# Feed-forward: the first products of two gate pairs ahead of four plain tiles made whole

## The chip, the cores and the metric

The kernel runs on one core of a Trainium2 chip. The time is device microseconds of one execution; the table below gives the median of three runs. The profile is of one further execution, whose own time stands beside its span.

The engines are named as the profile names them: PE (TensorE matmul), PEld (its weight load), DVE (VectorE), ACT (ScalarE), POOL (GpSimd) and SP (SyncE, which here only issues DMAs).

## What is computed

A small decoder trunk in float32: 512 tokens, width 1024, two layers (a short convolution, then windowed attention), and behind each a SwiGLU feed-forward of width 2816. The change lies in the feed-forward, which both layers run:

```python
def swiglu(h, w_gate_up, w_down):
    g, u = jnp.split(h @ w_gate_up, 2, axis=-1)
    return (jax.nn.silu(g) * u) @ w_down

ff = swiglu(rmsnorm(h, ffn_pre_norm[l]), ffn_w_gate_up[l], ffn_w_down[l])
h = h + rmsnorm(ff, ffn_post_norm[l])
```

## The kernel before

**Split numbers.** Every float32 operand of a matmul is split into a high part (ACT, a copy to fp32r) and a low part (DVE, the difference). A product is then three matmuls, hi·lo, hi·hi and lo·hi (`mm3`, L207 to L210). Where a token tile holds its high and low half side by side (`both`), one matmul of 512 columns does hi·[hi|lo], and one of 256 does lo·hi; the two halves of the PSUM bank are added afterwards. A weight block is 128x1024; it is loaded by SP into one of 7 `raw` buffers and split once.

**Tiles and pairs.** The 2816 gate and 2816 up columns are cut into 22 tiles of 128. The first two are "plain" (`PLAIN = 2`): two gate and two up tiles, each a sum over eight k-blocks of the normalised tokens. The other 20 come as ten pairs `q`. A pair is computed by a seven-product scheme: the 2x2 blocks of weights and tokens are combined so that seven block products (numbered 1 to 7) on 256 tokens each do for eight. Product 1 uses the first four k-blocks of the first 256 tokens, product 2 the last four of the same tokens; 6, 5, 7, 3 and 4 use sums of token quarters (`factors`, L389), for which all 512 tokens are needed.

**A pair in the code.** `gate_jobs` (L1203) makes seven jobs in the order 1, 2, 6, 5, 7, 3, 4. Products 1, 6, 7, 4 accumulate in the same two PSUM banks (chain X), one for each of two output tiles; 5 and 3 in Z; 2 in Y. Behind each product `take` (L1230) reads the bank: after product 1 ACT copies one half and DVE adds the other (`st`, 2 + 2 operations of 256 columns), after 6 the same, after 7 four DVE adds, after 4 two copies, two adds and two multiplies of 512; after 5 one ACT copy; after 2 and 3 one DVE add of 512. So product 6 adds onto the banks in which product 1 stands, and `take` reads the running sum. Matmuls of the next product of a chain must wait until `take` has read the bank. At pair 0 the first two products' weights were split beforehand.

**The order.** Everything in the feed-forward runs under a schedule written by hand: PE, DVE, ACT and POOL take their instructions in the order of the program. `in_line` (L505) runs the jobs: run job j (PE, then `take`), split the weights of job j + 3, add the raw blocks of job j + 4 where a pair's sums aren't ready made (L488), and emit one of the late parts. Late parts are the six steps by which a finished gate pair is turned into operands of the down projection (`pair_sums`, L601). Jobs of the first down projection take none at first. Ready-made sums of weight blocks are accumulated in HBM by POOL's DMAs (`sum_on`).

**The opening of a layer.** The stage before ends with the last token tile's norm, which is a long chain over DVE, POOL and ACT, and PE needs work that uses only the first 256 tokens until tiles 2 and 3 are done. `last_tile` (L1132) writes out that chain, with splits of the first tokens (`split`), copies of token quarters (`keep`) and two early weight splits (`weights`, in half blocks) between. `project_first` (L1158) gives PE its work: the four plain tiles on the first 256 tokens, k by k, then on the last 256. Between its k-blocks stand the transposes of tiles 2 and 3 (`turn`), the splits and copies of the last 256 tokens, and `factors`. After it, `late` closes the plain tiles (`gate_pair`: silu on ACT, multiply on DVE) and the jobs of the pairs begin.

```python
for hf in range(2):                                  # 256 tokens each
    for ks in ((0, 1), *((k,) for k in range(2, KT))):
        for ps, (whi, wlo) in zip(pss, ws):          # four plain tiles
            for k in ks:
                mm3(ps[:, c], ...)                   # N = 256
        for k in ks:
            then(hf, k)                              # turns, splits, factors
```

**Weights ahead.** `Ahead` holds the weights split before the layer begins: four are split while the stage before closes (`one`, whole blocks), two in `last_tile` (`slots`). Before, `first_weights` names the four of the plain tiles and then the two of pair 0's products 1 and 2.

Of the kernel before, what the change touches and what calls it, by code (L numbers as in the profile page):

```python
# [12 lines left out]
AF = mybir.ActivationFunctionType  # L13
ALU = mybir.AluOpType
PSUM = bass.MemoryType.PSUM

P = 128
# [5 lines left out]
ROUNDS = [(0, 6), (6, 10), (10, 14), (14, 18), (18, 22)]  # L23

PLAIN = 2

ADDED = (1, 2, 3, 4, 5, 7)

# [55 lines left out]
def yoco_kernel(  # L84
# [43 lines left out]
    def slot(s, dt=F32, w=S):  # L128
        return big.tile([P, w], dt, tag="slot", name=name(s), padded_shape=[P, S])
# [127 lines left out]
    class Update:  # L257
# [128 lines left out]
                else:  # L386
                    nc.scalar.activation(out, src, AF.Copy, scale=gain)

        def factors(self):  # L389


            x = self.x[0]
            made = {p: [] for p in range(1, 8)}
            for p, k0, c in ((1, 0, 0), (2, 4, 0), (3, 4, 256)):
                made[p] = [[a[:, c : c + 256] for a in x[k0 + k]]
                           + [two[:, :, c : c + 256] for two in self.both[k0 + k :][:1] if two]
                           for k in range(4)]
            for j in range(2):
                q11, q21, q12, q22 = (self.parts[i, hf, j] for hf in range(2) for i in range(2))

                nc.vector.tensor_tensor(out=q11, in0=q11, in1=q12, op=ALU.subtract)
# [730 lines left out]
    def last_tile(res, pieces, ahead=None):  # L1132


        def some(i):
            for n, *f in pieces[i]:
                if n == "keep":
# [20 lines left out]
    def project_first(pss, ws, x, then):  # L1158
        for hf in range(2):
            c = slice(hf * 256, (hf + 1) * 256)  # L1160

            for ks in ((0, 1), *((k,) for k in range(2, KT))):
                for ps, (whi, wlo) in zip(pss, ws):
                    for k in ks:
                        kk = slice(k * P, (k + 1) * P)
                        mm3(ps[:, c], whi[:, kk], wlo[:, kk],
                            x[k][0][:, c], x[k][1][:, c], k == 0, k == KT - 1)
                for k in ks:
                    then(hf, k)
# [12 lines left out]
    def ffn(l, before, ahead, gain, gpres, following):  # L1182
# [5 lines left out]
        def gate_pair(pg, pu):  # L1188
# [11 lines left out]
            pair.clear()  # L1200
            return pair_sums(gr, acts[0])

        def gate_jobs(q, factors, out, to, then):  # L1203


# [13 lines left out]
            split = {}  # L1219
            if q == 0:  # L1220

                pools = {"X": ps_sc, "Y": ps_pt, "V": ps_pt, "Z": ps_mm}
                raws[1], raws[2] = [], []
                split = {1: ahead.ready[4], 2: ahead.ready[5]}
            banks, kept = {}, []

            def tiles(a):
                return a.rearrange("p (e c) -> p e c", e=2)

            def take(p):  # L1230
                x, y, z, v = (banks.get(c) for c in "XYZV")
                st, u, gr = kept
                g0, g1 = (gr.rearrange("p (e h c) -> p e h c", e=2, h=2)[:, :, h]
                          for h in range(2))

                def add(out, a, b):
                    nc.vector.tensor_tensor(out=out, in0=a, in1=b, op=ALU.add)  # L1237
# [29 lines left out]
            def run(p):  # L1267
                def products(job):
                    if not kept:
                        kept.extend([slot("st"), slot("st"), wide("gr")])  # L1270
                    whi, wlo = split[p] if p in split else job.w
                    c = chain[p]
                    opened = c not in banks
                    if opened:
# [23 lines left out]
            def end():  # L1298
# [44 lines left out]

        acts = [[] for _ in ROUNDS]
        mix = [None] * NB
        pss = [bank("pgu", ps_mm) for _ in range(4)]
        with tc.manual_schedule(engines=ALL):
            last_tile(before, [
                [(0, 4)], [(0, 5), ("keep", 0, False), ("weights",)],
                [], [("keep", 1, True), (0, 6), (0, 7), ("keep", 3, True)],  # L1350
                [("keep", 2, False), ("weights",)]], ahead)

            def then(hf, k):
                if hf == 0 and k in (5, 6):
                    for b in ((0, 1), (2, 3))[k - 5]:
                        before.turn(b, (2,))
                if hf == 0 and k == 6:
                    for b in range(4):
                        before.turn(b, (3,))
                    for f in range(KT):  # L1360
                        before.split(0, f, 1)
                    for b in range(4):
                        before.keep(b, 1)
                if hf == 1 and k == 1:
                    factors.update(before.factors())
                if hf == 1 and k == 3:
                    if l == 0:
                        sum_on("o1")
                    sum_on(f"{l}f0")

            factors = {}
            project_first(pss, ahead.ready[:4], xs, then)

            def late():
                parts = [gate_pair(*pss[i : i + 2]) for i in (0, 2)][1]
                sum_on(f"{l}f1")
                return parts
# [568 lines left out]
```

## Time and profile before

| | |
|---|---|
| median of 3 runs | 1010.17 us (1009.65 to 1010.23) |
| the profiled execution | 1010.16 us, of which the span is 1008.3 us |
| mean granted TensorE clock | 0.998 |
| first feed-forward opens (first matmul of a plain tile) | 176.7 us, in layer 1 494.3 us later |

A profile line of a group reads: line, engine, operation, output <- inputs, shapes, count, then busy time and mean duration in ns of one, then the idle time before it and what ended that. A line of the timeline reads: start and duration in us, engine, line, operation, count, and in brackets the idle time before it with its releaser. Rows of several like instructions are merged (x8), and a duration overlaps the start of the next instruction, so that the step from start to start is what one costs on its engine. Line numbers such as L1237 are lines of the kernel; L1237 is the `add` inside `take`, L501 the low half of a weight split, L500 its high half, L192 and L198 the same for half blocks, L369 and L370 high and low of a token split, L387 a `keep`, L401 to L412 `factors`.

### The profile page before, as it was taken

How to read it: one execution, taken by the hardware profiler on the slowest of the kernel's cores; microseconds unless marked ns; L12 is line 12 of the kernel's file. 1: busy time of each engine (PE TensorE's matmuls, PEld its weight loads, DVE VectorE, ACT ScalarE, POOL GpSimd, SP SyncE). 2: the span in 40 equal slices, each digit the busy share in tenths (PEclk: the TensorE clock that was granted, in tenths of full speed). 3: DMA queues.
4: the chain of work that ended last, by engine and by line, in shares of the span. 5: the costliest groups of instructions: out<-in, count | busy, mean ns of one | idle time of the engine just before them, and what ended most of it. 6: DMA issues, size and time to landing. Idle time of an engine off the chain costs nothing. (4 is left out here: it accounts for less than half of the span.)

```text
span 1008.3 us, 16460 instructions
## 1 busy us (share of the span) xinstructions
PE 999.5 (99%) x6008; PEld 887.4 (88%) x6008; DVE 911.2 (90%) x1564; ACT 609.5 (60%) x1105; POOL 184.6 (18%) x250
## 2 busy tenths in 40 slices
PE   9999999999999999999999999999999999999997
PEld 8899888999889898898898888799998988989986
DVE  7898877899799999999888998989997999999996
ACT  7445545875655455566485788777666564646641
POOL 0211021212101011000022756321201010110001
PEclk9999999999999999999999999999999999999999
DMA  9885988669979699779504889966999587978742
GB/s 342 266 253 172 335 291 289 200 198 286 342 236 298 225 301 317 241 217 333 198 1 136 216 241 250 278 259 170 311 281 315 167 253 239 300 259 271 244 169 83
DMA packets 67872, 246.61 MB, mean 245 GB/s; under 512 B 8016, under 2 KB 8784, under 8 KB 56016
## 3 DMA queue, kind: packets, MB, share of 16 engines
q1 hardware_dynamic: 52624, 148.14, 39.5%
q0 software_dynamic: 14592, 96.48, 37.6%
q8 instruction: 47, 0.77, 0.3%
q10 hardware_dynamic: 576, 0.95, 0.3%
q14 instruction: 33, 0.27, 0.1%
HBM read 239.25 MB, written 102.76 MB: 339 GB/s over the span
## 5 line engine op out<-in xcount | busy, mean ns | idle before, releaser
L501 DVE TENSOR_TENSOR wlo<-raw,whi 128x1024 fp32r<-128x1024 f32 (+1 forms) x231 | 279.0, 1212 | 26.5 <-ACT whi L500 26.3
L500 ACT ACTIVATE whi<-raw 128x1024 fp32r<-128x1024 f32 (+1 forms) x231 | 239.7, 1051 | 79.1 <-DVE raw L488 37.6
L1282 PE MATMUL gx<-xt,whi 128*128 128x512 f32 x480 | 120.6, 393 | 0.0
L1282 PEld LDWEIGHTS gx<-xt,whi 128*128 128x128 f32 x480 | 86.2, 189 | 15.7
L571 POOL DMA_DIRECT2D hsum<-in_w_gb_dram x96 | 63.7, 727 | 160.8 <-ACT whi L500 107.5
L571 POOL DMA_DIRECT2D hsum<-hsum x32 | 25.3, 790 | 351.5 <-ACT whi L500 257.7
L1260 ACT ACTIVATE st<-gx 128x256 f32<-128x256 f32 x120 | 43.5, 380 | 60.8 <-PE gx L1285 57.2
L1237 DVE TENSOR_TENSOR st<-gx,st 128x256 f32<-128x256 f32 x200 | 77.4, 417 | 2.2 <-ACT st L1260 0.4
L1285 PEld LDWEIGHTS gx<-xt,wlo 128*128 128x128 f32 x480 | 65.5, 190 | 4.7
L1285 PE MATMUL gx<-xt,wlo 128*128 128x256 f32 x480 | 66.9, 282 | 0.0
L1296 ACT ACTIVATE gr<-gr 128x1024 f32<-128x1024 f32 x20 | 21.2, 1062 | 55.8 <-DVE gr L1237 55.8
L208 PE MATMUL gy<-xlo,whi 128*128 128x256 f32 x176 | 49.8, 283 | 0.0
L209 PE MATMUL gy<-xhi,whi 128*128 128x256 f32 x176 | 49.8, 283 | 0.0
L210 PE MATMUL gy<-xhi,wlo 128*128 128x256 f32 x176 | 49.8, 283 | 0.0
L208 PE MATMUL px<-wlo,ahi 128*128 128x512 f32 x120 | 46.7, 389 | 0.0
L209 PE MATMUL px<-whi,ahi 128*128 128x512 f32 x120 | 46.7, 389 | 0.0
L210 PE MATMUL px<-whi,alo 128*128 128x512 f32 x120 | 46.7, 389 | 0.0
L571 POOL DMA_DIRECT2D hsum<-in_w_dn_dram x48 | 32.1, 765 | 69.0 <-ACT whi L500 47.4
L1282 PE MATMUL gx<-xhl,whi 128*128 128x512 f32 x160 | 39.9, 391 | 0.0
L672 DVE TENSOR_TENSOR mix<-mix,px 128x512 f32<-128x512 f32 x54 | 34.8, 679 | 2.1 <-PE px L210 2.1
L318 POOL TENSOR_TENSOR ur<-uv,mhalf 128x1 f32<-128x1 f32 x15 | 13.9, 928 | 115.0 <-DVE uv L313 114.9
L488 DVE TENSOR_TENSOR raw<-raw,raw 128x1024 f32<-128x1024 f32 x28 | 34.1, 1218 | 0.1
(359 smaller groups left out, 3052.4 us busy)
## 6 DMA issues: line engine op xcount, KB each, us to landing
hsum<-in_w_gb_dram POOLq DMA_DIRECT2D x96, 512.0 KB, 8.0
raw<-hsum SPq DMA_DIRECT2D x88, 512.0 KB, 8.1
raw<-in_w_gb_dram SPq DMA_DIRECT2D x60, 512.0 KB, 7.1
hsum<-in_w_dn_dram POOLq DMA_DIRECT2D x36, 512.0 KB, 8.0
raw<-in_w_dn_dram SPq DMA_DIRECT2D x32, 512.0 KB, 7.0
hsum<-hsum POOLq DMA_DIRECT2D x28, 512.0 KB, 5.6
hsum<-in_w_dn_dram POOLq DMA_DIRECT2D x12, 768.0 KB, 13.0
raw<-in_w_in_dram SPq DMA_DIRECT2D x13, 512.0 KB, 7.2
```

Of the source, the lines that this page charges most:

```text
L208: nc.tensor.matmul(out, whi, xlo, start=start, stop=False, **kw)
L209: nc.tensor.matmul(out, whi, xhi, start=False, stop=False, **kw)
L210: nc.tensor.matmul(out, wlo, xhi, start=False, stop=stop, **kw)
L488: nc.vector.tensor_tensor(out=raw, in0=raw, in1=self.raws[1].tile, op=ALU.add)
L500: self.begun = nc.scalar.activation(hi[:, :n], raw, AF.Copy)
L501: nc.vector.tensor_tensor(out=lo[:, :n], in0=raw, in1=hi[:, :n].bitcast(F32), op=ALU.subtract)
L571: nc.gpsimd.dma_start(dst, src, max_dma_last_dim=4 * 4 * S, **kw))
L672: nc.vector.tensor_tensor(out=m, in0=m, in1=banks[bs][r], op=ALU.subtract if half else ALU.add)
L1237: nc.vector.tensor_tensor(out=out, in0=a, in1=b, op=ALU.add)
L1260: nc.scalar.activation(ste, a, AF.Copy)
L1282: nc.tensor.matmul(banks[c][e], whi[:, kk], factors[p][k][2], start=opened and k == 0, stop=False, **kw)
L1285: nc.tensor.matmul(banks[c][e][:, :256], wlo[:, kk], factors[p][k][0], start=False, stop=k == 3 and p in (4, 5), **kw)
```

## The change

Four weights are ready when the layer begins; now they are blocks 0 and 1 of pairs 0 and 1 (products 1 and 2), and the four of the plain tiles come later. PE's work on the first 256 tokens is now products 1 and 2 of both pairs (`Opening`), kept in four banks that hold product 1 and then product 1 + 2. Copies and adds bring these sums into SBUF (`st` and one half of `gr`). The plain tiles become four jobs at the head of the line, each made whole with 512 columns. The jobs of pairs 0 and 1 begin at product 6, in fresh banks, and `take` adds `st` where the bank no longer holds product 1.

```diff
+OPENED = 2
-        def factors(self):
+        def factors(self, between):
...
                     made[p] += [[hi[:, c : c + 256], lo[:, c : c + 256], two[:, :, c : c + 256]]
                                 for c in (0, 256)]
+                if j == 0:
+                    between()
             return made
...
     def first_weights(l):
-        return ([w_gu[l, f, j] for f in range(2) for j in range(2)]
-                + [w_gb[l, 0, b] for b in range(2)])
+        return ([w_gb[l, q, b] for b in range(2) for q in range(OPENED)]
+                + [w_gu[l, f, j] for f in range(PLAIN) for j in range(2)])
...
+        class Opening:
+            def __init__(self, q):
+                self.ws = ahead.ready[q], ahead.ready[OPENED + q]
+                self.x = [bank("gx", ps_mm) for _ in range(2)]
+                self.st, self.gr = slot("st"), wide("gr")
+
+            def one(self, k):
+                whi, wlo = self.ws[0]
+                for e, ps in enumerate(self.x):
+                    kk = slice(e * S + k * P, e * S + (k + 1) * P)
+                    nc.tensor.matmul(ps, whi[:, kk], before.both[k][:, :, :256], start=k == 0,
+                                     stop=False, skip_group_check=True)
+                    nc.tensor.matmul(ps[:, :256], wlo[:, kk], xs[k][0][:, :256], start=False,
+                                     stop=False, skip_group_check=True)
+
+            def two(self, *ks):
+                whi, wlo = self.ws[1]
+                for k in ks:
+                    for e, ps in enumerate(self.x):
+                        kk = slice(e * S + (k - 4) * P, e * S + (k - 3) * P)
+                        mm3(ps[:, :256], whi[:, kk], wlo[:, kk],
+                            *(a[:, :256] for a in xs[k]), False, k == KT - 1,
+                            skip_group_check=True)
+
+            def to(self, second, e):
+                return (self.gr[:, e * S : e * S + 256] if second
+                        else self.st[:, e * 256 : (e + 1) * 256])
+
+            def copy(self, second):
+                for e, ps in enumerate(self.x):
+                    nc.scalar.activation(self.to(second, e), ps[:, :256], AF.Copy)
+
+            def add(self, second):
+                for e, ps in enumerate(self.x):
+                    out = self.to(second, e)
+                    nc.vector.tensor_tensor(out=out, in0=ps[:, 256:], in1=out, op=ALU.add)
...
-                if p == 2:
+                if early and p == 6:
+                    both = slot("st")
+                    kept.append(both)
+                    for e in range(2):
+                        c = slice(e * 256, (e + 1) * 256)
+                        add(both[:, c], x[e][:, :256], st[:, c])
+                        add(both[:, c], x[e][:, 256:], both[:, c])
+                elif early and p == 5:
+                    add(u, z, st)
+                elif early and p == 3:
+                    add(g1, tiles(z), tiles(kept[3]))
+                elif early and p == 4:
+                    for e in range(2):
+                        c = slice(e * 256, (e + 1) * 256)
+                        add(st[:, c], x[e][:, :256], st[:, c])
+                        add(st[:, c], x[e][:, 256:], st[:, c])
+                elif p == 2:
                     add(g0, tiles(y), tiles(st))
...
-                    for p in (1, 2, 6, 5, 7, 3, 4)]
+                    for p in (1, 2, 6, 5, 7, 3, 4)[2 if early else 0 :]]
...
-        pss = [bank("pgu", ps_mm) for _ in range(4)]
         with tc.manual_schedule(engines=ALL):
+            ahead.fetch(2)
+            opened_pairs = first, second = [Opening(q) for q in range(OPENED)]
+            for pair_of in opened_pairs:
+                for k in range(4):
+                    pair_of.one(k)
             last_tile(before, [
-                [(0, 4)], [(0, 5), ("keep", 0, False), ("weights",)],
-                [], [("keep", 1, True), (0, 6), (0, 7), ("keep", 3, True)],
+                [(0, 4)],
+                [(0, 5), ("keep", 0, False), ("do", lambda: first.copy(False)),
+                 ("do", lambda: first.add(False))],
+                [("do", lambda: second.copy(False))],
+                [("keep", 1, True), (0, 6), (0, 7), ("keep", 3, True),
+                 ("do", lambda: second.add(False))],
                 [("keep", 2, False), ("weights",)]], ahead)
...
+            first.two(4, 5)
+            second.two(4, 5)
+            for b in range(2):
+                before.turn(b, (2,))
+            first.two(6, 7)
+            for b in range(2, 4):
+                before.turn(b, (2,))
+            for b in range(4):
+                before.turn(b, (3,))
+            first.copy(True)
+            first.add(True)
+            second.two(6, 7)
+            for f in range(KT):
+                before.split(0, f, 1)
+            ahead.slots()
+            second.copy(True)
+            second.add(True)
+            for b in range(4):
+                before.keep(b, 1)
+            ahead.one()
+            factors = before.factors(ahead.one)
+
+            pss = []
+
+            def plain_job(n):
+                def run(job):
+                    pss.append(bank("pgu", ps_mm))
+                    project(pss[n], ahead.ready[2 * OPENED + n], xs)
+
+                def then():
+                    if n == 0:
+                        if l == 0:
+                            sum_on("o1")
+                        sum_on(f"{l}f0")
+                    if n == 1:
+                        sum_on(f"{l}f1")
+                    return gate_pair(*pss[n - 1 :]) if n % 2 else None
+
+                return Job([], run, then)
...
-            jobs, behind_one = [], []
+            jobs, behind_one = [plain_job(n) for n in range(2 * PLAIN)], []
```

`project_first`, its `then` and the old `late` are removed; `project` (three matmuls of 512 columns for each of eight k-blocks) is the kernel's own, unchanged.

More of the change, by code (lines that the diff above doesn't have):

```diff
@@ L1136, in some @@
             for n, *f in pieces[i]:
-                if n == "keep":
+                if n == "do":
+                    f[0]()
+                elif n == "keep":
                     res.keep(f[0], 0, f[1])
@@ L1156, in last_tile @@
         some(4)
[L1158 to L1169, printed above, removed]
     def first_weights(l):
-        return ([w_gu[l, f, j] for f in range(2) for j in range(2)]
-                + [w_gb[l, 0, b] for b in range(2)])
+        return ([w_gb[l, q, b] for b in range(2) for q in range(OPENED)]
+                + [w_gu[l, f, j] for f in range(PLAIN) for j in range(2)])
     sum_on("o0")
@@ L1218, in gate_jobs @@
             pools = {"X": ps_mm, "Y": ps_pt, "V": ps_pt, "Z": ps_sc}
-            split = {}
             if q == 0:
                 pools = {"X": ps_sc, "Y": ps_pt, "V": ps_pt, "Z": ps_mm}
-                raws[1], raws[2] = [], []
-                split = {1: ahead.ready[4], 2: ahead.ready[5]}
             banks, kept = {}, []
+            early = opened_pairs[q] if q < OPENED else None
             def tiles(a):
@@ L1231, in take @@
                 x, y, z, v = (banks.get(c) for c in "XYZV")
-                st, u, gr = kept
+                st, u, gr = kept[:3]
                 g0, g1 = (gr.rearrange("p (e h c) -> p e h c", e=2, h=2)[:, :, h]
@@ L1269, in products @@
                     if not kept:
-                        kept.extend([slot("st"), slot("st"), wide("gr")])
-                    whi, wlo = split[p] if p in split else job.w
+                        kept.extend([early.st, slot("st"), early.gr] if early
+                                    else [slot("st"), slot("st"), wide("gr")])
+                    whi, wlo = job.w
                     c = chain[p]
@@ L1345, in ffn @@
         mix = [None] * NB
-        pss = [bank("pgu", ps_mm) for _ in range(4)]
         with tc.manual_schedule(engines=ALL):
-            last_tile(before, [
-                [(0, 4)], [(0, 5), ("keep", 0, False), ("weights",)],
-                [], [("keep", 1, True), (0, 6), (0, 7), ("keep", 3, True)],
-                [("keep", 2, False), ("weights",)]], ahead)
[L1353 to L1372, printed above, removed]
+            ahead.fetch(2)
@@ L1374, in late @@
             def late():
-                parts = [gate_pair(*pss[i : i + 2]) for i in (0, 2)][1]
-                sum_on(f"{l}f1")
-                return parts
-            jobs, behind_one = [], []
+                return []
+            jobs, behind_one = [plain_job(n) for n in range(2 * PLAIN)], []
             for rd, (f0, f1) in enumerate(ROUNDS):
```

## The prediction

> **What bounds the kernel now.** I read the page first (span, busy shares), then busy time by windows, then the timelines of PE, DVE and ACT around the start of the first feed-forward layer.
>
> ```profile
> span 1008.3 us, 16460 instructions
> PE 999.5 (99%) x6008; PEld 887.4 (88%) x6008; DVE 911.2 (90%) x1564; ACT 609.5 (60%) x1105; POOL 184.6 (18%) x250
> ```
>
> PE is never idle for long, so the first question is what one matmul costs. A listed duration overlaps the next one; the step from start to start is the price.
>
> ```profile
> 166.09 0.39 PE L208 MATMUL pmix<-wlo,yhi 128*128 128x512 f32 x1
> ...
> 173.34 0.39 PE L210 MATMUL pmix<-whi,ylo 128*128 128x512 f32 x1
> ...
> 176.70 0.28 PE L208 MATMUL pgu<-xhl,whi 128*128 128x256 f32 x1
> ...
> 189.95 0.28 PE L208 MATMUL pgu<-xhl,whi 128*128 128x256 f32 x1
> ...
> 201.47 2.00 PE L1282 MATMUL gx<-xhl,whi 128*128 128x512 f32 x8
> ```
>
> From 166.09 to 173.34 lie 32 steps of 512 columns: 0.2266 us each. From 189.95 to 201.47 lie the 96 matmuls of 256 columns of the second half of the plain tiles: 0.120 us each. Two halves cost 0.013 us more than a whole.
>
> But PE is not alone at its limit. The windows below are the gate pairs right behind the plain tiles, in layer 0 and, 494 us later, in layer 1 (columns: PE, PEld, DVE, ACT, POOL busy, clock, DMA share, GB/s).
>
> ```profile
> 215.00:264.00 49.00, 49.00 (x333) 45.41 (x332) 48.62 (x78) 31.38 (x48) 8.12 (x14) 1.00 0.84 276
> 709.00:758.00 49.00, 49.00 (x333) 45.49 (x332) 48.62 (x77) 31.69 (x48) 7.58 (x12) 1.00 0.95 301
> ```
>
> DVE is busy 48.62 of 49 us, in both layers, beside a full PE. Its rows stand without a gap:
>
> ```profile
> 226.93 1.21 DVE L501 TENSOR_TENSOR wlo<-raw,whi 128x1024 fp32r<-128x1024 f32 x1
> 228.06 0.41 DVE L614 TENSOR_TENSOR a<-gr,a 128x256 fp32r<-128x256 f32 x1
> 228.39 0.68 DVE L1237 TENSOR_TENSOR gr<-gy,st 128x512 f32<-128x512 f32 x1
> 228.99 1.21 DVE L501 TENSOR_TENSOR wlo<-raw,whi 128x1024 fp32r<-128x1024 f32 x1
> 230.13 1.21 DVE L488 TENSOR_TENSOR raw<-raw,raw 128x1024 f32<-128x1024 f32 x1
> 231.26 0.41 DVE L617 TENSOR_TENSOR s<-gr 128x256 f32<-128x256 f32 x1
> 231.71 0.43 DVE L618 SCALAR_TENSOR_TENSOR s<-s,gr 128x256 f32<-128x256 f32 x1
> 232.05 0.75 DVE L1237 TENSOR_TENSOR st<-gx,st 128x256 f32<-128x256 f32 x2
> 232.72 1.21 DVE L501 TENSOR_TENSOR wlo<-raw,whi 128x1024 fp32r<-128x1024 f32 x1
> ...
> 236.26 1.66 DVE L1237 TENSOR_TENSOR st<-gx,st 128x256 f32<-128x256 f32 x4
> 237.84 1.21 DVE L501 TENSOR_TENSOR wlo<-raw,whi 128x1024 fp32r<-128x1024 f32 x1
> ```
>
> These rows also price DVE, from start to next start: a 1024-wide split or raw sum 1.13, a 512-wide operation 0.60, one 256-wide 0.33, two 256-wide adds 0.67, four 1.58, a subtract with its partner (L617, L618) 0.79. Where the two engines meet is shown by pair 2:
>
> ```profile
> 251.96 0.75 DVE L1237 TENSOR_TENSOR st<-gx,st 128x256 f32<-128x256 f32 x2
> 252.44 1.87 PE L1282 MATMUL gx<-xt,whi 128*128 128x512 f32 x7
> ```
>
> Product 7 adds onto the banks X of product 6, so PE may write them only once DVE has read them. The first of the two adds ends near 252.37 (half of 0.75 after 251.96), and product 7 starts at 252.44. The slack is about 0.1 us: whatever makes DVE later here makes PE later.
>
> The Trainium skill, Perfetto Trace Analysis, "Identifying the Most-Contended Engine", says not to judge TensorE by its matmul occupancy but by its weight loads, and VectorE by occupancy. By that, the page's 90% of DVE stand above the 88% of PEld; the windows agree, and the rule speaks against trading PE time for DVE time.
>
> **The change, part by part** (one layer; times of layer 0).
>
> *Plain tiles whole.* 192 matmuls of 256 columns go (192 x 0.120 = 23.0 us), 96 of 512 come (96 x 0.2266 = 21.8): PE does 1.3 us less. The opening's products 1 and 2 are the same matmuls as before, 8 of 512 and 32 of 256 columns for each pair, and the 16 transposes only move; so PE's gain is 1.3 us a layer, 2.5 in all.
>
> The Trainium skill, TensorE: Matmul & The Clock Gate, "Back-to-back issue gap", gives N/2.4 + 2.5 ns, 109 and 216 ns for the two widths. By it the gain would be an estimated 0.2 us a layer; the rows here, 120 and 227 ns, decide for 1.3.
>
> *DVE's work.* Each opened pair loses its products' place in the banks, so their sums are added by hand. Product 6: four adds for a copy on ACT and two adds, 1.58 - 0.67 = +0.9. Product 5: a 512-wide add in place of ACT's copy, +0.6. Product 4: +0.9 as for 6. Product 2: two 256-wide adds for one 512-wide, +0.1. That is 2.5 a pair, **5.0 us of DVE a layer**. ACT loses five copies a pair and gains two; at 31 of 49 us it bounds nothing. Weight splits only move: pair 1's first two (2 x 1.13) from the pairs' stage to the opening.
>
> *DVE's waits in the opening.* Here I walk the queues, since ACT and DVE take their work in the order written.
>
> ```profile
> 186.24 1.14 ACT L192 ACTIVATE whi<-raw 128x512 fp32r<-128x512 f32 x2
> 188.06 1.57 ACT L369 ACTIVATE xhl<-xt,gt 128x256 fp32r<-128x256 f32 x4 [0.67 <-PE xt L356]
> 189.50 1.59 ACT L369 ACTIVATE xhi<-xt,gt 128x256 fp32r<-128x256 f32 x4
> 190.93 3.08 ACT L387 ACTIVATE part<-xt,gt 128x256 f32<-128x256 f32 x8
> ...
> 201.94 1.04 ACT L500 ACTIVATE whi<-raw 128x1024 fp32r<-128x1024 f32 x1
> ```
>
> ```profile
> 182.19 1.28 DVE L198 TENSOR_TENSOR wlo<-raw,whi 128x512 fp32r<-128x512 f32 x2
> ...
> 186.90 1.29 DVE L198 TENSOR_TENSOR wlo<-raw,whi 128x512 fp32r<-128x512 f32 x2 [0.74 <-ACT whi L192]
> 188.57 1.66 DVE L370 SCALAR_TENSOR_TENSOR xhl<-xt,gt,xhl 128x256 fp32r<-128x256 f32 x4 [0.38 <-ACT xhl L369]
> 190.14 1.65 DVE L370 SCALAR_TENSOR_TENSOR xlo<-xt,gt,xhi 128x256 fp32r<-128x256 f32 x4
> 192.22 0.69 DVE L401 TENSOR_TENSOR part<-part,part 128x512 f32<-128x512 f32 x1 [0.42 <-ACT part L387]
> ...
> 197.61 0.68 DVE L401 TENSOR_TENSOR part<-part,part 128x512 f32<-128x512 f32 x1
> ...
> 203.01 1.22 DVE L501 TENSOR_TENSOR wlo<-raw,whi 128x1024 fp32r<-128x1024 f32 x1
> 204.93 1.29 DVE L1196 TENSOR_TENSOR gr<-pgu,gr 128x512 f32<-128x512 f32 x2 [0.69 <-ACT gr L1195]
> ...
> 214.60 1.23 DVE L501 TENSOR_TENSOR wlo<-raw,whi 128x1024 fp32r<-128x1024 f32 x1 [1.14 <-ACT whi L500]
> ```
>
> After, up to 182 nothing of weight changes: an early split gives way to two copies and two adds. ACT (steps: a half split 0.53, a 256-wide copy 0.38, eight pieces 2.9, eight keeps 3.0, a 1024-wide split near 1.0): weights' high half at 186.5, first pair's copies 187.5, eight high pieces 188.3 to 191.1, the next weights to 192.2, second pair's copies to 192.9, the eight keeps to 195.9, and only then the new split, to 197.0. DVE: low half to 188.3, first pair's adds to 189.0, eight low pieces to 192.2, weights to 193.4, second pair's adds to 194.1, and then it waits for that split from 194.1 to 197.0: **2.9 us idle**, with the factors queued behind. Then a split to 198.1, half the factors (192.22 to 197.61, 5.4) to 203.5, a split to 204.7, the other half to 210.1. So the first split of pair 0, at 203.01 before, starts at 210.1.
>
> PE in the opening: from 176.7 the products 1 of both pairs take 2 x (8 x 0.2266 + 8 x 0.120) = 5.5, the products 2 5.8, the transposes 1.7 us as before (189.95 - 176.70 - 96 x 0.120); plain tiles start near 189.8, where the first low piece (189.5) and the first weights (188.4) are just ready, and end near 211.5. Their third and fourth weights (198.1, 204.7) come 2 us before use. No PE wait is costed, with 0 as the lower bound and 1.0 us, about half that margin, as the upper.
>
> *From there to pair 2's product 6*, DVE does, after: 15 splits and 4 raw sums at 1.13 (21.5), two gate products (1.2), six fours of adds (9.5), four multiplies behind product 4 (2.4), four 512-wide adds (2.4), pair 2's products 1 and 2 (1.3), two sets of six pair-sum parts (0.33 + 2 x 0.79 + 3 x 0.60 = 3.7 each, 7.3), and waits for the table and ACT 1.1: 46.7, so it gets there at 256.8. The same count for before, with 17 splits, six twos and two fours of adds, two parts more (1.1) and waits of 1.8, gives 48.4 where the trace has 251.96 - 203.01 = 48.95, so the prices hold to 0.5. DVE is **4.8 us later** (256.8 against 251.96). Without the waits: 5.0 of work, less 1.1 of parts that slip behind this point, plus some 1.2 of waits, less small change.
>
> PE, 1.2 us early at the end of pair 0's first products, stalls at the banks of products 7 and 4 in pairs 0 to 2, and stands 4.8 us later at pair 2's product 7. Afterwards the gap is not made good: PE has no wait of its own to lose, while DVE recovers in the first down projection:
>
> ```profile
> 270.97 3.50 DVE L501 TENSOR_TENSOR wlo<-raw,whi 128x1024 fp32r<-128x1024 f32 x3 [3.67 <-ACT whi L500]
> ```
>
> That idle time of DVE takes up the late parts; PE's delay stays. Two more fetches of 512 KB a layer (pair 1's blocks come twice) are costed at nothing: the window's DMA share is 0.84, the raws are asked for 8 us or more ahead; uncovered they would cost at most one split's lead of 1.1 us. On SP the two extra fetches go out at the layer's start, ahead of tile 3's store; on POOL the block sums of f0 and f1 hang on plain tiles 0 and 1, within 2 us of where they stood. Both are costed at nothing: DVE, which would show such a wait first, has no gap in the rows above.
>
> *Sum.* Both layers have the same DVE share, so 2 x 4.8 = 9.6 us. The profiled execution took 1010.16 us (span 1008.3 and 1.9 around it), the median of the runs is 1010.17: **1019.8 us**.
>
> **Rivals.**
> 1. *PE alone decides* (the other side). If DVE's 5.0 us found cover, only PE's gain would be left: 1010.2 - 2.5 = 1007.6. It decides once DVE has over 6 us a layer of slack ahead of product 7; the 0.1 us there and 48.62 of 49 us speak against it. For it speaks only that PE has 99%. 10%.
> 2. *The opening's wait vanishes.* If the new split's high half were done before the keeps, DVE would not idle 2.9 us; 4.8 - 2.9 = 1.9 a layer, 1014.0. For it: ACT has idle time around 187. Against: the order is written out. 17%.
> 3. *The opening starves PE too*: plain weights or low pieces over 0.3 to 2 us late, or ACT's copies in the way of the last tile's norm. Twice 1 to 2 us on top: near 1023. 8%.
> 4. *Balance*: half the additions hidden, stalls equal to the gain, within 2 us of before. 5%.
>
> **How the numbers follow.** Forecast 60%, its own range 1016.5 to 1022.5 (the 0.5 us of the check, the 1.0 and the fetches, for each layer). With rival 2 below it and part of 3 above, 1012.5 to 1023.5 holds 8 in 10. A measurement of this kernel can tell about 0.2% (2 us) from no change. Faster by more: rival 1, 10%. Within: rival 4 and a sliver of 2, 6%. Slower: 84%.
>
> **What would show it.** Right: 5816 matmuls, plain tiles at 0.227 us a step; DVE waiting 2 to 3 us for ACT's whi ahead of the factors near 194; the first DVE split of pair 0 near 210; PE gaps of 0.5 to 4 us at products 7 and 4 of pairs 0 to 2; pair 2's product 7 near 257 in place of 252.4, and the same in layer 1. Wrong: DVE idle in those pairs, PE without gaps there, or the two layers moving differently; then the end comes near 1007.6, or the loss sits in the opening.

## The result and the profile after

The changed kernel took **1027.49 us** (median of 5 runs, 1024.67 to 1028.10), beside 1010.05 for the kernel before on the same chip: a ratio of 1.0167, 95% interval 1.0151 to 1.0182. That is 17.4 us slower, where 9.6 were forecast. The sign and most of the mechanism held; the size did not, and it lies above the range.

The page of the changed kernel, its span and busy shares:

```profile
span 1025.7 us, 16087 instructions
PE 1004.4 (98%) x5816; PEld 881.9 (86%) x5816; DVE 920.5 (90%) x1588; ACT 603.5 (59%) x1093; POOL 184.4 (18%) x250
```

192 matmuls are gone, as counted, and DVE's busy time grew by 9.3 us (920.5 - 911.2), near the 10.0 of the forecast. PE's busy time *rose* by 4.9 us, though it has less to do. That is the first sign of something the forecast lacks. A sum of busy time grows without more work when matmuls take longer. So I read the opening next, PE's timeline and then the windows (columns: PE, PEld, DVE, ACT, POOL busy, clock, DMA share, GB/s).

```profile
183.49 0.28 PE L210 MATMUL gx<-xlo,whi 128*128 128x256 f32 x1
...
185.88 0.36 PE L210 MATMUL gx<-xlo,whi 128*128 128x256 f32 x1 [1.87 <-ACT part L389]
...
188.89 0.41 PE L210 MATMUL gx<-xlo,whi 128*128 128x256 f32 x1
...
189.53 0.41 PE L210 MATMUL gx<-xlo,whi 128*128 128x256 f32 x1
...
193.55 0.40 PE L210 MATMUL pgu<-xhl,whi 128*128 128x512 f32 x1
```

```profile
184.00:186.00 2.00, 0.13 (x2) 0.15 (x2) 2.00 (x6) 2.00 (x5) 2.00 (x5) 1.00 0.89 66
186.00:188.00 2.00, 2.00 (x15) 2.00 (x16) 1.36 (x3) 0.88 (x2) 1.22 (x3) 0.84 0.68 139
188.00:190.00 2.00, 2.00 (x12) 2.00 (x11) 0.00 (x0) 0.00 (x0) 0.00 (x0) 0.50 1.03 213
190.00:192.00 2.00, 2.00 (x16) 2.00 (x16) 0.85 (x2) 1.11 (x3) 0.00 (x0) 0.81 0.97 287
```

PE stops at 183.85 and starts again at 185.88, at product 2 of the second pair. Three matmuls from 188.89 to 189.53 then take 0.213 us each, where 0.120 is the price: the granted clock has fallen to 0.50. So the plain tiles begin at 193.55 and not near 189.8, and ACT and DVE, which follow PE there, are as late. The Trainium skill, TensorE: Matmul & The Clock Gate, "Part 1: The HAM clock gate", states that the clock falls to half after at least one idle window of about 3.4 us, and that the windows run free of the kernel. The trace agrees on the half clock; on the length it differs, here 2.0 us of idle time were enough.

What PE waited for stands in DVE's timeline; L1231 is the `add` of `Opening`.

```profile
184.54 0.86 DVE L386 TENSOR_SCALAR part<-xt,gt 128x256 f32<-128x256 f32 x2
185.32 0.75 DVE L1231 TENSOR_TENSOR st<-gx,st 128x256 f32<-128x256 f32 x2
...
200.17 1.23 DVE L447 TENSOR_TENSOR wlo<-raw,whi 128x1024 fp32r<-128x1024 f32 x1 [2.92 <-ACT whi L442]
...
213.28 1.23 DVE L505 TENSOR_TENSOR wlo<-raw,whi 128x1024 fp32r<-128x1024 f32 x1
...
231.45 1.66 DVE L1265 TENSOR_TENSOR st<-gx,st 128x256 f32<-128x256 f32 x4
...
249.74 1.67 DVE L1265 TENSOR_TENSOR st<-gx,st 128x256 f32<-128x256 f32 x4
...
260.33 0.75 DVE L1265 TENSOR_TENSOR st<-gx,st 128x256 f32<-128x256 f32 x2
```

The first of the adds at 185.32 ends near 185.7, and PE starts at 185.88. Its bank is the one that product 2 adds onto, so PE cannot write it sooner. (The bracket on PE's row names ACT's `part`, the last semaphore by the profile; experiment e1 shows that DVE's add decides.) DVE's own stages are as forecast: it waits 2.92 us for ACT's `whi` behind the keeps (2.9 forecast), and from its first split of pair 0 (213.28) to pair 2's product 6 (260.33) it needs 47.05 us (46.7 forecast).

Then the pairs, PE's timeline and its waits (columns of the second: us in all, times, longest; L1327 is the first matmul line of products 6 and 7, L1265 the `add` in `take`):

```profile
238.32 3.55 PE L1327 MATMUL gx<-xt,whi 128*128 128x512 f32 x8 [2.75 <-DVE st L1265]
...
254.93 2.11 PE L1327 MATMUL gx<-xt,whi 128*128 128x512 f32 x8 [0.67 <-DVE st L1265]
```

```profile
PE gx L1327 <- DVE st L1265: 8.1, 4, 2.8
PE gx L210 <- ACT part L389: 3.8, 2, 1.9
```

PE waits at product 7 of pair 1 and at product 6 of pair 2, in both layers; the forecast had named products 7 and 4 of pairs 0 to 2. Behind the first of these waits in layer 0 the clock falls again, to 0.51 from 240 to 242 us: eight matmuls take 3.55 us, where like eight take 2.11. In layer 1 a wait of the same 2.75 us at the same place (ahead of 741.38) is followed by 1.00 and by eight in 2.06 us. Pair 2's product 7 starts at 260.80 in place of 252.44. Of these 8.4 us nothing is made good or added later in the layer; the next layer's 8.7 come the same way (763.85 against 746.75).

### The profile page after: what moved, and what is told of

Same layout as the page of the kernel before. It is cut to its first block, busy times and chain, and to the rows that moved or that the text cites. A ratio compares the mean times of both kernels' runs of the same rounds, so it can differ in the third digit from the quotient of the medians.

```text
span 1025.7 us, 16087 instructions
## 1 busy us (share of the span) xinstructions
PE 1004.4 (98%) x5816; PEld 881.9 (86%) x5816; DVE 920.5 (90%) x1588; ACT 603.5 (59%) x1093; POOL 184.4 (18%) x250
## 5 line engine op out<-in xcount | busy, mean ns | idle before, releaser
L505 DVE TENSOR_TENSOR wlo<-raw,whi 128x1024 fp32r<-128x1024 f32 (+1 forms) x227 | 274.4, 1214 | 23.4 <-ACT whi L504 23.3
L504 ACT ACTIVATE whi<-raw 128x1024 fp32r<-128x1024 f32 (+1 forms) x227 | 234.7, 1050 | 98.2 <-DVE raw L492 56.5
L1327 PE MATMUL gx<-xt,whi 128*128 128x512 f32 x480 | 122.6, 398 | 8.1 <-DVE st L1265 8.1
L1327 PEld LDWEIGHTS gx<-xt,whi 128*128 128x128 f32 x480 | 87.1, 190 | 25.4 <-ACT whi L504 5.8
L1265 DVE TENSOR_TENSOR st<-gx,st 128x256 f32<-128x256 f32 x208 | 81.3, 419 | 2.7 <-ACT st L1304 0.4
L1304 ACT ACTIVATE st<-gx 128x256 f32<-128x256 f32 x96 | 34.7, 380 | 52.1 <-PE gx L1330 42.7
L210 PE MATMUL px<-wlo,ahi 128*128 128x512 f32 x120 | 46.7, 389 | 0.0
L211 PE MATMUL px<-whi,ahi 128*128 128x512 f32 x120 | 46.7, 389 | 0.0
L212 PE MATMUL px<-whi,alo 128*128 128x512 f32 x120 | 46.7, 389 | 0.0
L210 PE MATMUL gy<-xlo,whi 128*128 128x256 f32 x144 | 40.8, 283 | 0.0
L211 PE MATMUL gy<-xhi,whi 128*128 128x256 f32 x144 | 40.8, 283 | 0.0
L212 PE MATMUL gy<-xhi,wlo 128*128 128x256 f32 x144 | 40.7, 283 | 0.0
L447 DVE TENSOR_TENSOR wlo<-raw,whi 128x1024 fp32r<-128x1024 f32 x18 | 21.7, 1222 | 13.0 <-ACT whi L442 12.9
```

What stands on the lines that cost most here:

```text
L210: nc.tensor.matmul(out, whi, xlo, start=start, stop=False, **kw)
L211: nc.tensor.matmul(out, whi, xhi, start=False, stop=False, **kw)
L212: nc.tensor.matmul(out, wlo, xhi, start=False, stop=stop, **kw)
L504: self.begun = nc.scalar.activation(hi[:, :n], raw, AF.Copy)
L505: nc.vector.tensor_tensor(out=lo[:, :n], in0=raw, in1=hi[:, :n].bitcast(F32), op=ALU.subtract)
L1304: nc.scalar.activation(ste, a, AF.Copy)
```

## The experiments

**What the opening's wait costs.** In e1, DVE reads the second pair's banks ahead of the keeps and splits of its list. In e6, PE waits as before, but is kept busy with four transposes of tile 2, done five times over.

```diff
 e1
-                [("keep", 1, True), (0, 6), (0, 7), ("keep", 3, True),
-                 ("do", lambda: second.add(False))],
+                [("do", lambda: second.add(False)),
+                 ("keep", 1, True), (0, 6), (0, 7), ("keep", 3, True)],
 e6
+            for _ in range(5):
+                for b in range(2):
+                    before.turn(b, (2,))
             second.two(4, 5)
-            for b in range(2):
-                before.turn(b, (2,))
```

> Only the place of the second pair's first two adds changes: ahead of the keeps and token splits instead of behind them. Theory (PE waits in the opening because product 2 of the second pair adds onto banks that DVE has not read): the 1.9 us wait near 185.9 and the half clock behind it go, the plain tiles start near 189.5 instead of 193.6, DVE starts pair 0's first weight split 3 us sooner, and the time falls by 2 x 3.2 to about 1021 us. Rival (the wait is for the keeps and the weight split on ACT, as its label says): the wait stays and the time stays near 1027.5.

> The changed kernel with tile 2's transposes for banks 0 and 1 set ahead of the second pair's product 2 and done five times over, so that PE computes through its 2 us wait. Theory (the granted clock falls because PE stood idle about 2 us, and the slow matmuls behind it cost as much again as half the wait): the clock stays at 1.00 from 186 to 192, the twelve matmuls of the first pair's product 2 take 1.5 instead of 2.7 us, the plain tiles start 1 to 1.5 us sooner and the time falls by 2 to 3 us, to about 1025. Rival (the slow stretch comes from data arriving late, not from the clock): no change, or slower by the added transposes.

e1: **1020.36 us** (1019.88 to 1021.49), ratio 1.0106 (1.0091 to 1.0121). e6: 1023.50 (1023.45 to 1024.99), ratio 1.0139 (1.0124 to 1.0154). PE's waits in e1, and the windows of e6:

```profile
PE gx L1327 <- DVE st L1265: 8.1, 4, 2.8
```

```profile
186.00:188.00 2.00, 2.00 (x19) 2.00 (x18) 1.29 (x2) 0.65 (x2) 0.99 (x3) 1.00 0.71 147
188.00:190.00 2.00, 2.00 (x20) 2.00 (x20) 0.79 (x2) 1.22 (x4) 0.00 (x0) 1.00 1.05 217
```

In e1 the row of 3.8 us is gone, and DVE's add was the only thing moved. That is worth 7.1 us (1027.49 - 1020.36), twice the 3.8 that the row shows. e6 tells why: its PE reaches the second pair's product 2 as late as ever (185.72 against 185.88) and still the kernel is 4.0 us faster, with a clock of 1.00.

The clock does not fall every time. In the profiled execution of e2 (below; its opening is the changed kernel's) PE waits as long, and the clock stays at 1.00:

```profile
184.00:186.00 2.00, 0.33 (x3) 0.36 (x4) 1.86 (x6) 2.00 (x5) 2.00 (x6) 1.00 0.08 12
188.00:190.00 2.00, 2.00 (x20) 2.00 (x19) 0.70 (x2) 0.85 (x3) 0.00 (x0) 1.00 1.07 221
```

This divides the 7.1 us. From the first matmul of product 2 to the first plain tile PE takes 11.24 us in the changed kernel (182.31 to 193.55), with the wait and the slow clock; 9.69 in e2 (182.10 to 191.79), with the wait alone; 7.59 in e1 (182.22 to 189.81), with neither. So in a layer the wait costs 2.1 us and the slow clock 1.55, and layer 1 gives the same: 4.2 and 3.1 us, 7.3 in all. e6 takes 9.33 (182.09 to 191.42): it saves the slow clock and 0.36 us for four transposes that now stand in the wait.

**Which of DVE's delays counts in the pairs.** What is left in e1, 10.5 us over before, is close to the 9.6 forecast. The forecast put it on 5.0 us of added sums and 2.9 us of waiting for a late split in each layer. e3 takes away the wait (the split's high half stands ahead of the keeps on ACT); e2 takes away the sums; e7 both.

```diff
 e3 (on top of e1)
+            ahead.hi()
             for b in range(4):
                 before.keep(b, 1)
-            ahead.one()
+            ahead.lo()
 e2 (e7: e2 and e3)
-                if early and p == 6:
+                if early and p == 6 and False:
...
-                elif early and p == 5:
+                elif early and p == 5 and False:
...
-                    add(g1, tiles(z), tiles(kept[3]))
-                elif early and p == 4:
+                    add(g1, tiles(z), tiles(st))
+                elif early and p == 4 and False:
```

> Sooner reading as in e1_read_sooner, and the high half of the first whole plain weight split stands ahead of the eight keeps on ACT, not behind them. Theory (what DVE waits for in the opening is paid in full at pair 2): DVE's 2.9 us wait for that split goes, the time falls from 1020.4 by 2 x 2.9 to about 1014.6. Rival (the rest of the loss is the DVE work in the pairs alone): 1020 stays.

> Leaves out the adding of product 1's sum behind products 6, 5, 3 and 4 of pairs 0 and 1; a copy on ACT stands there again, as in the kernel before. The matmuls are the changed kernel's. Theory (DVE has no slack there, so its added work is paid in full): 2.3 us less DVE work a pair, the wait at pair 1's product 7 (2.8 us, and slow clock behind it) goes, 4.6 us a layer, time near 1018. Rival (the loss lies in the opening alone): 1027.5 less at most 1 us.

> As e3_split_sooner, and the adding of product 1's sum behind products 6, 5, 3 and 4 of pairs 0 and 1 left out (copies on ACT in its place). Theory: DVE is then hardly later than in the kernel before, PE has no wait in the pairs, and what is left is PE's own gain of 2 x 1.3 us: 1007.4. Rival (whole tiles gain nothing on PE, or the opening still costs): 1010 or above.

e3: 1020.18 us (1018.81 to 1020.59), ratio 1.0100 (1.0085 to 1.0116). e2: 1024.06 (1021.62 to 1026.92), ratio 1.0142 (1.0117 to 1.0167). e7: 1017.67 (1017.22 to 1018.67), ratio 1.0079 (1.0065 to 1.0093). All three fell short; e3 gained nothing that can be told from e1. DVE's timeline of e3:

```profile
206.52 1.23 DVE L505 TENSOR_TENSOR wlo<-raw,whi 128x1024 fp32r<-128x1024 f32 x1
...
213.91 1.67 DVE L1265 TENSOR_TENSOR st<-gx,st 128x256 f32<-128x256 f32 x4 [1.53 <-PE gx L1330]
```

DVE's first split of pair 0 came 3.0 us sooner than in e1 (209.56), as planned. But then DVE stood still for PE, which was busy with the plain tiles and had not made product 6 yet. Splits are made three jobs ahead only, so DVE could not use the time. The head start of 3.0 us was down to 1.1 at pair 2's product 6 (250.15 against 251.22), and a new wait in the first down projection of layer 0 (1.4 us, `px` for DVE's `mix`) took that back: at the layer's last pair e3 stands at 468.42, e1 at 468.22. e2 (which leaves the sums out) stood 4.9 us ahead of the changed kernel at pair 2's product 7 of layer 0 (255.89 against 260.80). But 1.8 of these it had already at the first plain tile (191.79 against 193.55), where its clock had not fallen; the sums are worth the other 3.1, and 3.3 were lost again by the last pair (469.90 against 471.47), 2.6 of them in a wait for `mix`. Its runs (1021.62 to 1026.92) overlap the changed kernel's, so its gain is not clear. Its mean granted clock was 0.998 in the fastest and 0.994 in the two slowest of them, so the clock's fall may be what sets them apart.

So I asked how much work each engine has per pair. The row of 28 us below is the same stretch, pairs 0 to 2, in four kernels: before, after, e3, e7.

```profile
222.00:250.00 28.00, 28.00 (x194) 26.11 (x193) 27.83 (x44) 17.05 (x27) 6.60 (x10) 1.00 0.80 239
```

```profile
222.00:250.00 28.00, 25.25 (x156) 22.70 (x155) 27.56 (x47) 11.70 (x14) 3.45 (x5) 0.94 0.89 272
```

```profile
222.00:250.00 28.00, 23.94 (x160) 21.73 (x158) 27.45 (x47) 14.25 (x20) 5.23 (x8) 1.00 0.81 246
```

```profile
222.00:250.00 28.00, 26.14 (x170) 23.53 (x169) 27.64 (x46) 17.08 (x28) 4.87 (x8) 1.00 0.80 249
```

Before, both engines were full. In the three others DVE is as full as it was and PE is short by 2 to 4 us: the pairs have become DVE's stage. (In the changed kernel a part of PE's 25.25 is slow clock, 0.94.) The rows at 231.45 and 249.74 above give its price. They are the adds behind product 4 of pairs 0 and 1, one whole pair apart, and DVE has no wait between them: **18.3 us of DVE for a pair, while PE's five products take 14.2** (two take 5.67, 246.77 to 252.44 in the trace of before). Without the sums, in e7, it is still more than PE's:

```profile
227.41 0.75 DVE L1265 TENSOR_TENSOR st<-gx,st 128x256 f32<-128x256 f32 x2
...
243.42 0.75 DVE L1265 TENSOR_TENSOR st<-gx,st 128x256 f32<-128x256 f32 x2
```

16.0 us a pair against 14.2. That would explain why leaving the sums out did not bring the time back. Products 1 and 2 keep PE busy for 5.7 us a pair, but ask little of DVE: two splits and three adds, 2 x 1.13 + 0.67 + 0.60 = 3.5 us. With them a pair is in balance: 16.0 + 3.5 = 19.5 us of DVE beside seven products of 2.83, 19.8 us of PE, which is the full window of before. (Five jobs emit five late parts and seven jobs all six; with the sixth, some 0.6 us, it is about 20. DVE's rows of before at 232.05 and 251.96, product 6 of pairs 1 and 2, are 19.9 us apart.) By these prices they were the cover under which DVE caught up with the other five. Taken out and done early, they leave the pairs short of PE work even without the sums. e7 stands at 253.49 for pair 2's product 7, 1.05 us behind before, and its layer 0 loses 3.9 more behind it (467.99 against 463.08 at the last pair). Part of that is the wait for `mix`:

```profile
PE gx L1327 <- DVE st L1265: 3.6, 4, 1.4
PE px L210 <- DVE mix L676: 2.5, 1, 2.5
```

ACT's next weights for the down projection come late from DMA there (a wait of 3.91 us for `raw` ahead of 282.38). Why these DMAs are late was not tried.

**DVE's work alone.** e5 leaves the kernel before as it is and gives DVE four 512-wide adds into a spare slot in pairs 0 and 1 each, 4.8 us a layer.

```diff
+                spare = slot("spare") if q < 2 and p in (5, 6, 7, 4) else None
+                if q < 2 and p in (5, 6, 7, 4):
+                    add(spare, st, st)
```

> The kernel before with four extra 512-wide adds into a spare tile behind products 6, 5, 7 and 4 of pairs 0 and 1, 0.60 us each, 4.8 us of DVE work a layer, nothing else changed. Theory (no slack): up to 1.8 us go into DVE's waits of 0.7 and 1.1 us in pair 0, the rest shows, 3.0 to 4.8 us a layer: 1016 to 1020 us, with PE waits at product 7 of pairs 1 and 2. Rival (DVE's work there is covered by the three jobs' lead of the weight splits): within 1 us of 1010.

1024.57 us (1023.58 to 1026.48), ratio 1.0147 (1.0130 to 1.0164): 14.7 us for 9.6 us of DVE. So the 0.1 us of slack read before the change was real: DVE's time is paid in full here, and half as much again, which is more than the 3.0 to 4.8 us a layer that I had expected. PE's waits and two of its rows:

```profile
PE gx L1285 <- DVE st L1238: 10.4, 9, 1.9
```

```profile
229.08 3.49 PE L1285 MATMUL gx<-xt,whi 128*128 128x512 f32 x8 [1.88 <-DVE st L1238]
...
253.17 3.66 PE L1285 MATMUL gx<-xt,whi 128*128 128x512 f32 x8 [1.86 <-DVE st L1238]
```

The waits sum to 10.4 us, near the 9.6 that were added. The rest has the signature of the opening: eight matmuls that take about 3.5 us in place of 2.1 behind a wait of 1.9, with a granted clock of 0.50 from 230 to 232 and from 254 to 256 us.

**Moving DVE's work to POOL.** e4 is e3 with the low halves of the pair sums of the plain pair and pairs 0 and 1 on POOL, nine 512-wide subtracts a layer; e8 is the control, the same move in the kernel before.

```diff
-    def pair_sums(gr, to):
+    def pair_sums(gr, to, eng=nc.vector):
...
-            nc.vector.tensor_tensor(out=lo, in0=src, in1=hi.bitcast(F32), op=ALU.subtract)
+            eng.tensor_tensor(out=lo, in0=src, in1=hi.bitcast(F32), op=ALU.subtract)
```

> As e3_split_sooner, and the low halves of the pair sums of the plain pair and of pairs 0 and 1 are made on POOL instead of DVE: nine operations of 0.60 us a layer, six of them ahead of pair 2's product 6. Theory (DVE's work there decides until PE does): 3.6 us a layer less, which passes the point at which PE decides, so the PE gain of 1.3 us a layer shows: 1007.4 to 1010. Rival (POOL and DVE disturb each other, or POOL's queue of sums falls behind): 1012 or more.

> The kernel before with the low halves of the pair sums of the plain pair and of pairs 0 and 1 on POOL, as a control for e4_splits_on_pool. Theory (before, PE decides and DVE just keeps up): 1010, within 1 us. Rival (DVE already bounded the kernel before): 2 us or more faster.

e4: 1025.05 us (1024.47 to 1026.48), ratio 1.0153 (1.0139 to 1.0167), 4.9 us *slower* than e3 with 18 DVE operations fewer. e8: 1013.21 (1012.96 to 1013.67), ratio 1.0034 (1.0022 to 1.0047). So the move costs 3.5 us by itself (1013.21 - 1009.74), and the waits of e8 show it as DVE's lateness:

```profile
PE gx L1282 <- DVE st L1237: 2.3, 3, 0.9
```

DVE was not relieved. A weight split that takes 1.21 us elsewhere takes up to 4.31 in e8 where POOL's subtracts run beside it (L624 is the subtract, L501 the split):

```profile
236.47 4.31 DVE L501 TENSOR_TENSOR wlo<-raw,whi 128x1024 fp32r<-128x1024 f32 x1
236.62 1.31 POOL L624 TENSOR_TENSOR alo<-s,ahi 128x512 fp32r<-128x512 f32 x1
238.38 1.31 POOL L624 TENSOR_TENSOR alo<-gr,ahi 128x512 fp32r<-128x512 f32 x1
```

The 229 splits of L501 take 14.3 us more in e8 than before (291.9 against 277.6), while the 18 subtracts that left DVE are 10.8 us of work (18 x 0.60). DVE's busy time rose by 3.4 us, from 911.2 to 914.6, and from e3 to e4 by 6.3, from 920.5 to 926.8. So e4 says nothing against DVE as the bound: it loads DVE further. Why a split is slower beside POOL's subtracts was not tried.

**Where PE's cover stands.** If DVE is short of PE cover in the pairs, part of the plain tiles could stand there. e9 is e3 with the fourth plain tile behind product 6 of pair 0, e11 with the same tile behind product 5, e10 is e9 without the sums. (One or two jobs take two late parts, so that the first down projection finds its operands.)

```diff
+                    if q == 0:
+                        jobs.insert(4, jobs.pop(3))       # e11: insert(5, ...)
```

> The edit of e3, and the fourth plain tile stands behind product 6 of pair 0 instead of ahead of it. Theory (VectorE bounds the stage from its first split of pair 0 on): in e3 it did that split at 206.52 us, then needed 5.3 us of work up to 213.91, where it waited 1.53 for PE, and 41.6 us from there to pair 2's product 7. Now PE ends product 6 earlier, so the wait goes, but product 6 itself waits about 1.5 us for its weights (206.2 to 207.7). 206.5 + 5.3 + 41.6 + about 1 = 254.4 for pair 2's product 7, against 256.02 in e3: 1.6 a layer, 1017 us. Rival 1 (the order of the tiles is what binds, and PE decides once it is mended): near 1008 to 1010. Rival 2 (nothing there matters, the loss is elsewhere): 1020 as e3.

> The edit of e9, and the additions of product 1's sum to products 6, 5, 3 and 4 are left out (ACT copies stand there as in pair 2), so 5 us less work for VectorE a layer. Theory: VectorE would reach pair 2's product 7 at 249.5, PE at about 251, so PE decides there for the first time: 251 in place of 253.5 in e7, 2.5 us a layer less than e7's 1017.7, 1012.7 us; what is then left above 1007.6 is lost behind the pairs, in the first down projection. Rival (the order is what bound, not VectorE's work): the same as e9.

> The edit of e3, and the fourth plain tile stands behind product 5 of pair 0, one job later than in e9. In e9 VectorE took up pair 0 early (products 6 read at 210.64 us in place of 213.91), then waited 0.72 and 2.11 us for PE, which stood in the fourth plain tile while the sum behind product 5 headed VectorE's queue; from 218.10 to pair 2 it had no gap. Theory (VectorE's queue is taken in order and bounds the stage as soon as it is never short of work): with product 5 ahead of the tile both waits go, VectorE works without a gap from 206.6, and pair 2's product 7 comes near 254.4 where e3 has 256.02 and e9 257.18: 1.6 a layer less than e3, 1017 us. If the placing of the tile binds otherwise: 1020 to 1023, as e3 and e9. In no case below 1012, since VectorE's 46.9 us of work from its first split on stay.

e9: 1022.64 us (1020.65 to 1023.80), ratio 1.0125 (1.0108 to 1.0142). e10: 1020.42 (1019.54 to 1021.37), ratio 1.0105 (1.0090 to 1.0120). e11: 1021.25 (1019.53 to 1022.50), ratio 1.0110 (1.0093 to 1.0127). None gained. DVE's rows, first of e9, then of e11:

```profile
215.30 0.69 DVE L1189 TENSOR_TENSOR gr<-pgu,gr 128x512 f32<-128x512 f32 x1 [0.72 <-PE pgu L212]
218.10 0.69 DVE L1265 TENSOR_TENSOR st<-gz,st 128x512 f32<-128x512 f32 x1 [2.11 <-PE gz L212]
```

```profile
218.15 0.69 DVE L1189 TENSOR_TENSOR gr<-pgu,gr 128x512 f32<-128x512 f32 x1 [1.27 <-PE pgu L212]
220.37 1.67 DVE L1265 TENSOR_TENSOR st<-gx,st 128x256 f32<-128x256 f32 x4 [1.52 <-PE gx L1330]
```

Each order moves DVE's idle time instead of filling it: 2.8 us in both, at other rows. A whole tile is 5.4 us of PE with at most one gate product for DVE behind it, and DVE, which takes its queue in order and has splits for three jobs only, runs dry under it; after its last wait it is full up to pair 2, and PE waits. e9's window of 222 to 250 us says the same as e3's, PE 24.77 beside DVE 27.42. Pair 2's product 7 came at 257.18 in e9 and 256.59 in e11, where e3 has 256.02.

No kernel tried beat the one before.

## Why the forecast was wrong in size

- **PE's own gain: right.** 96 matmuls from 193.55 on, 0.227 us a step; 1.3 us a layer less work.
- **DVE's added work: right.** 9.3 us more busy time, 10.0 forecast; 47.05 us for the stage, 46.7 forecast. The wait of 2.9 us ahead of the factors came to 2.92. (One small sum is off: half of 0.75 after 251.96 is 252.34 and not 252.37; the slack stays about 0.1 us.)
- **"No PE wait is costed, with 0 as the lower bound and 1.0 us, about half that margin, as the upper": the step that failed.** For the opening I checked what product 2 *reads*, low pieces and weights, and not the banks it *writes*. The second pair's `add(False)` stands last in DVE's list; the walk of the queues gave the first sums one clause ("an early split gives way to two copies and two adds") and set no time for the second pair's against PE. The wait came to 2.1 us a layer, and the slow clock behind it to 1.55 where it fell; e1 prices both at 7.1 us in all. With that measured term the sum would have been 9.6 + 7.1 = 16.7, against 17.4. Rival 3 had named other reasons for a starved PE (plain weights, low pieces, ACT's copies) and priced it at 1 to 2 us a layer, which holds for the wait, for another reason, and misses the clock.
- **Pair 2's product 7 about 4.8 us late a layer: right once the opening is mended.** In e1 DVE's first split of pair 0 stands at 209.56 (210.1 forecast) and product 7 at 257.09, 4.65 us behind before. The gaps that add up to it stand at other places than forecast, none of them in pair 0 or at a product 4. But the list of what makes it up ("5.0 of work", "plus some 1.2 of waits") read as terms that can be taken away one by one, and rival 2 priced the kernel without DVE's wait for the late split at 1014.0. e3 took that wait away and came to 1020.18. The waits and the sums are not separate terms: DVE's time in the pairs counts from product 6 of pair 0 on, which PE reaches only behind four whole tiles, and from there a pair asks 18.3 us of DVE and 14.2 of PE. That DVE's excess is 4.1 a pair and not 2.5 is what the list hid: the other 1.6 is by the prices above the loss of products 1 and 2, 5.7 us of PE beside 3.5 of DVE and a late part of some 0.6 that slips.
- **"PE alone decides" (1007.6): wrong, as thought likely.** It would take DVE's 18.3 us a pair below 14.2; even without the sums it is at 16.0.
- **The fetches, SP's and POOL's queues, costed at nothing:** no wait of PE names them, and ACT's waits for blocks split ahead of a layer grew by 0.9 us only (7.9 against 7.0). In the down projection of e7 a DMA wait appears; in the changed kernel itself the delay at pair 2 (8.4 us) is the delay at the layer's last pair (471.47 against 463.08), so there they cost nothing.

What stays open: when the clock falls behind such a wait and when it does not; the down projection's 3.9 us in e7; and why POOL's subtracts slow DVE's splits. That products 1 and 2 were DVE's cover rests on the prices above and on the full and empty windows; no kernel put them back into the pairs one at a time.

## What to carry to other kernels

Before work is moved out of a stage, count per unit of the loop what it asks of *each* engine. Work that is long on one engine and light on another is the cover for its neighbours, and gathering it in one place leaves both places unbalanced, with neither able to lend. The Trainium skill, Perfetto Trace Analysis, "Optimization Strategy", says that interleaving stretches with different contended engines may help; this change is the reverse of it, and the windows from 222 to 250 us show the price. And for each product that adds onto a bank, check who still has to read the bank, at which place in that engine's queue, not only whether its operands are ready.

## What was not expected of the hardware

- A wait of about 2 us on PE cost 1.55 us more through the granted clock: 0.50 from 188 to 190 us, and in layer 1 again from 690 to 692. It does not always: in the profiled execution of e2 the same wait left the clock at 1.00. With the wait filled with transposes (e6) the clock stood at 1.00 in both layers and the kernel gained 4.0 us, though the product behind them started no sooner.
- Eighteen 512-wide subtracts moved from DVE to POOL slowed the kernel before by 3.5 us (e8), though POOL is busy for 21% of the span only: beside them, single DVE splits took 1.7 to 4.3 us in place of 1.2, and DVE's busy time rose.
